# Seven places of weights and projection inputs, each at its own offset modulo 256 bytes

## The chip, the cores and the metric

The kernel runs on one core of a Trainium2 chip. The metric is the device time of one execution in microseconds; the time before is the median of three runs. The profile is one further execution, taken by the hardware profiler.

## The reference

A decoder trunk of two layers over 1024 tokens of width 1024, all in float32. Each layer mixes the tokens with three groups of heads side by side:

```
mod = SiLU(c) @ W_mod + b_mod;  shift, scale, gate = split(mod)
h = RMSNorm_pre(x) * (1 + scale) + shift
proj = h @ W_in                      # 1024 x 3088, split into the inputs of three groups
  A: sliding-window attention (window 128, 8 heads, 2 key/value heads, rotary, sinks)
  B: retention (4 heads, chunks of 128, own rotation and decay)
  C: gated linear attention (4 heads, low-rank data-dependent decay)
every group's output * SiLU(its gate path); B and C RMS-normalised per head first
y = concat(A, B, C) @ W_out          # 1024 x 1024
x = x + gate * RMSNorm_post(y)
```

## The kernel before

**Two halves of a number.** The large products (h @ W_in and the mix @ W_out) run in float32r, TensorE's one-pass form of a four-byte number. To keep float32's accuracy each operand is split into a high part (rounded to float32r) and a low part (the rest), and three products are added: high by high, low by high, high by low. In the code this is `PASSES = ((0, 0), (1, 0), (0, 1))`, over which `accum` loops, and inside it over eight blocks k of 128 rows of the contraction; so a product has 24 matmuls into one PSUM tile `mm`, each with another stationary operand of 128x128. Every matmul goes through the helper `mult` (line 171), every transpose through `transp` (line 186).

**Seven places.** Weights and projection inputs live in two long SBUF tiles, `arena0` and `arena1`, cut into seven places: 0, 1 and 2 in arena0, 3 to 6 in arena1. A place holds both halves of a weight unit of 256 columns (`unit`), or both halves of the transposed input h of two token tiles (`hT`): 2 x 8 rows of 256 four-byte numbers in each partition, 16384 bytes. Places 0 and 2 are wider (17408 bytes) since the unit rv has 16 more columns and is kept with rows of 272 numbers, 1088 bytes. `place(i)` gives the view of a place; the table `PLACES` has the tile, the offset in four-byte elements and the width of each. `TOK` says which places hold h in each layer (1, 2, 3, 4 in the first, 3, 4, 0, 1 in the second), `PLACE` which unit of weights goes where: rv, gg, gqk, aq0 and ag1 into place 0 (layer 0) or 2 (layer 1); rg, rk, gv, aq1 and o2 into 5; rq, kv, ag0 and o3 into 6; o0 and o1 into the first two places of h, once h is done with.

**Which operand moves.** `project` streams 256 columns of one unit (272 for rv) against h of one token tile; `project2` streams two units of 256 columns each as one moving operand of 512, joined by `both`, which steps from one place to the other; `project_T` streams h of two places (512 tokens) against 128 columns of a unit; `y_half` streams two units of W_out against `mx`, the mix of one token tile as read back from HBM (`load_mix`). In the last two token tiles of layer 1 the mix lies in a place of h instead. So in all of these the moving operand and the stationary one come from two different places, or from one or two places and mx.

**Where tiles stand.** SBUF is given out by pools that lie one above the other in each partition: const, big (arena0), work, and on top, once the start is over, big1 (arena1); a pool first, for the first modulation weights `wm`, has the room of arena1 before. The work pool has the working tiles: `sm` (small columns), `t1`, `kT`, `mx`, `t2` (14 buffers of 128x512), `acc`, `st` (staging of weights), `smx` and others. Two tiles that nothing reads or writes take up room alone: `pad` in const (96 bytes a partition) and `padw` in work (320 bytes). With them every place, and t1, kT, mx, t2, acc and st too, begin at multiples of 256 bytes.

**Order.** TensorE's instructions are in an order that the kernel writes out itself: the main loop issues the projections one product after another, and after every few matmuls `pump` lets waiting jobs (rotary, retention, attention, gates) issue their matmuls when a planner's clock says that they are due. The planner's clock and its latencies (table `L`) are constants of the program. The loads of weights (`load`) go through SP's queue into `st`; ScalarE and VectorE write the high half into its place and VectorE or GpSimd the low half (line 508).

Of the kernel before, what the change touches and what calls it, by code (L numbers as in the profile page):

```python
# [10 lines left out]
F32 = mybir.dt.float32  # L11
F32R = mybir.dt.float32r
# [5 lines left out]
P = 128  # L18
# [24 lines left out]

SLOT = KT * 512
WIDE = KT * 544
PLACES = {0: (0, 0, 272), 1: (0, WIDE, 256), 2: (0, WIDE + SLOT, 272)}
PLACES.update({3 + i: (1, i * SLOT, 256) for i in range(4)})
TOK = ((1, 2, 3, 4), (3, 4, 0, 1))
PLACE = []
for _t, _w in zip(TOK, (0, 2)):  # L50
# [39 lines left out]
def trunk(ctx: ExitStack, tc: tile.TileContext, ins, cst, out):  # L90
# [8 lines left out]
    bp = ctx.enter_context(tc.tile_pool(name="big", bufs=1))  # L99
    gp = ctx.enter_context(tc.tile_pool(name="work", bufs=2))  # L100
    ps = ctx.enter_context(tc.tile_pool(name="psum", bufs=3, space=bass.MemoryType.PSUM))
    dr = ctx.enter_context(tc.tile_pool(name="dram", bufs=1, space=bass.MemoryType.DRAM))

    gp.tile([P, 80], F32, tag="pad", name="padw", bufs=1)
    uid = [0]

    def nm(s):
# [21 lines left out]
    def f(ap):  # L129
        return ap.bitcast(F32)  # L130

    arenas = [bp.tile([P, 2 * WIDE + SLOT], F32R, name="arena0")]

    def place(i, w=256):
        n, o, _ = PLACES[i]
        return arenas[n][:, o:o + 2 * KT * w].rearrange("p (a k n) -> p a k n", a=2, k=KT)
# [623 lines left out]
    with tc.tile_pool(name="first", bufs=1) as wp:  # L760
        mod_first(rws, between)
    ap = ctx.enter_context(tc.tile_pool(name="big1", bufs=1))
    arenas.append(ap.tile([P, 4 * SLOT], F32R, name="arena1"))
    if XF:
        for t in (2, 3):
            load_x(t, xe[t], nc.sync)
# [540 lines left out]
    def load_mix(l, t):  # L1307
# [6 lines left out]
        if l == DEPTH - 1 and t in MIXP:  # L1314
            n, o, _ = PLACES[TOK[l][t // 2]]
            o += t % 2 * 2 * KT * P
# [323 lines left out]
```

## Time and profile before

| | |
|---|---|
| median of 3 runs | 957.99 us (956.76 to 958.2) |
| profiled execution | 954.65 us |
| its span | 952.9 us |
| granted TensorE clock | 0.997 |
| TensorE busy (matmul) | 932.7 us, 98% |
| weight loads | 770.1 us, 81% |
| VectorE, ScalarE, GpSimd | 67%, 50%, 23% |
| DMA | 142.26 MB, 149 GB/s in the mean |

Busy times are unions of an engine's instructions; since matmuls are pipelined, the time of one (its mean in ns) is longer than the step from one to the next. PE stands for TensorE's matmuls, PEld for its weight loads, DVE for VectorE, ACT for ScalarE, POOL for GpSimd, SP for the queue of SyncE.

### The profile page before, as it was taken

To read this page: it belongs to the slowest core of one execution; us is meant where nothing else is said; L and a number is where in the kernel's file an instruction comes from. 1 tells how busy PE (TensorE), PEld (TensorE's weight loads), DVE (VectorE), ACT (ScalarE), POOL (GpSimd) and SP (SyncE) were. 2 spreads that over 40 slices of the span, in tenths; PEclk is the share of its full clock that TensorE was granted. 3 is DMA by queue.
4 is the path that set the end of the run, shared out by engine and by line. 5 is a ranking of instruction groups with operands and counts; after the bars stand their busy time and mean duration, and the time that the engine had idled before them with its cause. 6 is when DMAs were issued, how large, how long until landed. Compare 5 with 4: busy or idle time off the path is not lost.

```text
span 952.9 us, 15951 instructions
## 1 busy us (share of the span) xinstructions
PE 932.7 (98%) x5645; PEld 770.1 (81%) x5645; DVE 637.4 (67%) x1372; ACT 474.1 (50%) x1157; POOL 222.6 (23%) x288
## 2 busy tenths in 40 slices
PE   5999999999999999999999999999999999999997
PEld 1799887888888787778889888888888887787886
DVE  6886857757786988654685584694677787862332
ACT  3786233554756666622455532443667576661111
POOL 3222000423231324510131110033133033540000
PEclk9999999999999999999999999999999999999999
DMA  9943523613362345787455261362133222555951
GB/s 320 323 135 122 161 84 122 196 49 115 107 200 80 100 133 189 226 253 256 171 169 175 92 187 32 101 187 67 56 101 111 94 82 81 166 177 177 308 200 66
DMA packets 124651, 142.26 MB, mean 149 GB/s; under 512 B 11566, under 2 KB 95384, under 8 KB 124572
## 3 DMA queue, kind: packets, MB, share of 16 engines
q1 hardware_dynamic: 114396, 127.43, 42.1%
q10 hardware_dynamic: 10176, 13.82, 4.2%
q8 instruction: 44, 0.72, 0.3%
q14 instruction: 35, 0.29, 0.1%
HBM read 104.51 MB, written 36.70 MB: 148 GB/s over the span
## 4 chain that ended last, share of the span: by engine, by line
PE 85%; DVE 3%; issue 2%; ACT 2%; POOL 0%; DMA 0%; DVEq 0%; SPq 0%; POOLq 0%; ACTq 0%
PE mm L171 67%; PE aux L171 14%; PE aux L186 4%; ACT smx L971 0%; DMA t<-tabS 0%; ACT L1026 0%; DVE t L856 0%; ACT L1025 0%; DVE t L1029 0%; DVE t L1027 0%; DVE t L157 0%; ACT mx L1160 0%; DVE smx L966 0%; DVE arena L508 0%; DVE arena L149 0%
## 5 line engine op out<-in xcount | busy, mean ns | idle before, releaser
L171 PE MATMUL mm<-arena,arena 128*128 128x512 f32 (+2 forms) x1512 | 309.6, 358 | 0.0
L171 PE MATMUL mm<-arena 128*128 128x512 f32 (+2 forms) x1392 | 285.8, 359 | 0.0
L171 PEld LDWEIGHTS mm<-arena,arena 128*128 128x128 f32 x1512 | 246.5, 189 | 40.1 <-issue 2.1
L171 PEld LDWEIGHTS mm<-arena 128*128 128x128 f32 x1392 | 228.9, 190 | 37.2 <-issue 1.2
L171 PE MATMUL mm<-arena,mx 128*128 128x512 f32 (+1 forms) x696 | 157.3, 384 | 0.0
L171 PEld LDWEIGHTS mm<-arena,mx 128*128 128x128 f32 x696 | 126.5, 188 | 26.1 <-issue 1.5
L508 POOL TENSOR_TENSOR arena<-st,arena 128x512 fp32r<-128x512 f32 x57 | 85.9, 1512 | 158.0 <-ACT arena L147 100.3
L147 ACT ACTIVATE t<-aux 128x512 f32<-128x512 f32 x64 | 37.1, 591 | 82.6 <-PE aux L186 39.6
L508 DVE TENSOR_TENSOR arena<-st,arena 128x512 fp32r<-128x512 f32 x63 | 63.0, 1014 | 6.9 <-ACT arena L147 3.5
L147 ACT ACTIVATE arena<-st 128x512 fp32r<-128x512 f32 x82 | 48.4, 623 | 31.1 <-PE mm L171 15.0
L1285 ACT ACTIVATE t<-mm 128x512 f32<-128x512 f32 x30 | 17.9, 598 | 91.0 <-PE mm L171 46.3
L971 ACT ACTIVATE smx<-smx,sm 128x129 f32<-128x129 f32 x128 | 50.1, 394 | 18.1 <-DVE sm L968 17.9
L975 POOL TENSOR_TENSOR smx<-smx,sm 128x512 f32<-128x512 f32 x32 | 35.2, 1099 | 82.5 <-DVE sm L974 78.7
L384 DVE SCALAR_TENSOR_TENSOR acc<-st,c_act,acc 128x512 f32<-128x512 f32 x60 | 45.6, 760 | 13.1 <-DMA st<-in_w_mod_dram 12.1
L562 POOL TENSOR_TENSOR sm<-sm,few 128x1 f32<-128x1 f32 x26 | 14.8, 570 | 150.3 <-DVE sm L561 147.6
L1286 DVE TENSOR_TENSOR t<-mm,modg 128x512 f32<-128x512 f32 x30 | 20.7, 689 | 42.4 <-ACT t L1285 42.4
L1330 DVE SCALAR_TENSOR_TENSOR t<-t,sm,t 128x512 f32<-128x512 f32 x32 | 25.5, 827 | 30.8 <-DMA t<-xs 15.7
L186 PE MATMUL aux<-c_ident,t 128*128 128x128 f32 x224 | 33.7, 274 | 4.1 <-DVE t L634 2.3
L186 PEld LDWEIGHTS aux<-c_ident,t 128*128 128x128 f32 x224 | 26.6, 140 | 10.5 <-DVE t L634 2.7
L966 DVE COPY_PREDICATED smx<-c_curmask,aux 128x256 f32<-128x256 int32 x64 | 25.5, 447 | 12.8 <-ACT smx L147 11.4
L370 POOL MEMSET acc<- 128x512 f32 x4 | 2.1, 529 | 130.2 <-PE aux L171 119.1
L851 DVE TENSOR_TENSOR t<-mm,sincos 128x128 f32<-128x128 f32 (+2 forms) x36 | 16.2, 450 | 23.7 <-ACT t L147 12.5
(223 smaller groups left out, 1340.5 us busy)
## 6 DMA issues: line engine op xcount, KB each, us to landing
st<-in_w_in_dram SPq DMA_DIRECT2D x96, 256.0 KB, 3.9
st<-in_w_mod_dram SPq DMA_DIRECT2D x64, 256.0 KB, 3.0
mixS<-t SPq DMA_DIRECT2D x64, 256.0 KB, 2.5
mx<-mixS SPq DMA_DIRECT2D x28, 512.0 KB, 5.2
st<-in_w_out_dram SPq DMA_DIRECT2D x32, 256.0 KB, 3.2
wm<-in_w_mod_dram SPq DMA_DIRECT2D x12, 512.0 KB, 4.7
t<-in_x_dram SPq DMA_DIRECT2D x24, 256.0 KB, 4.9
t<-tabS SPq DMA_DIRECT2D x16, 256.0 KB
```

Of the source, the lines that this page charges most:

```text
L147: A.activation(dst, src, AF.Copy)
L171: T.matmul(dst, lhsT, rhs, start=start, stop=stop)
L186: T.transpose(dst, src, idn)
L384: V.scalar_tensor_tensor(acc, wt, c_act[:, k:k + 1], acc, ALU.mult, ALU.add)
L508: i = (G if first == 0 and kc in LOG else V if first == 0 else eng(f"wlo{kc}")).tensor_tensor(wt[:, 1, 2 * kc:2 * kc + 2, 0:256], st, f(hi ...
L851: V.tensor_tensor(a4, s4, cs.unsqueeze(1).unsqueeze(1).to_broadcast((P, nh, 2, 32)), ALU.mult)
L966: V.copy_predicated(sv, curmask.unsqueeze(1).to_broadcast((P, 2, P)), pv[:, :, n // P - 1, :])
L971: A.activation(sm[:, h, :], sm[:, h, :], AF.Exp, bias=mx[:, h:h + 1], accum_out=sums[:, h:h + 1])
L975: eng("pn").tensor_tensor(sm[:, :, 0:128], sm[:, :, 0:128], rs.unsqueeze(2).to_broadcast((P, 4, P)), ALU.mult)
L1285: A.activation(yg, pm, AF.Square, accum_out=ss[:, nh:nh + 1])
L1286: V.tensor_tensor(yg, pm, modg[l][:, 512 * nh:512 * nh + 512], ALU.mult)
L1330: V.scalar_tensor_tensor(xt[j], yg[j], r, xt[j], ALU.mult, ALU.add)
```

## The change

The offsets of the seven places get an addend, given in four-byte elements (`SHIFT`): 0, 4, 8, 12, 24, 28 and 60, which is 0, 16, 32, 48, 96, 112 and 240 bytes. arena0 is 8 elements longer and arena1 60. The tile `padw` of 320 bytes is dropped from the work pool, and a tile `pad1` of 32 bytes is put ahead of arena1. So arena0 and arena1 themselves still begin at multiples of 256 bytes, and the working tiles in between come 288 bytes lower.

```diff
 SLOT = KT * 512
 WIDE = KT * 544
-PLACES = {0: (0, 0, 272), 1: (0, WIDE, 256), 2: (0, WIDE + SLOT, 272)}
-PLACES.update({3 + i: (1, i * SLOT, 256) for i in range(4)})
+SHIFT = (0, 4, 8, 12, 24, 28, 60)
+PLACES = {0: (0, 0, 272), 1: (0, WIDE + SHIFT[1], 256), 2: (0, WIDE + SLOT + SHIFT[2], 272)}
+PLACES.update({3 + i: (1, i * SLOT + SHIFT[3 + i], 256) for i in range(4)})
...
-    gp.tile([P, 80], F32, tag="pad", name="padw", bufs=1)
...
-    arenas = [bp.tile([P, 2 * WIDE + SLOT], F32R, name="arena0")]
+    arenas = [bp.tile([P, 2 * WIDE + SLOT + 8], F32R, name="arena0")]
...
     ap = ctx.enter_context(tc.tile_pool(name="big1", bufs=1))
-    arenas.append(ap.tile([P, 4 * SLOT], F32R, name="arena1"))
+    ap.tile([P, 8], F32, name="pad1")
+    arenas.append(ap.tile([P, 4 * SLOT + 60], F32R, name="arena1"))
```

## The prediction

> **What bounds the kernel now.** I read the page first (busy times, clock, chain), then who waits for TensorE's operands, then the groups by shape, then single runs of matmuls in the timeline.
>
> ```profile
> span 952.9 us, 15951 instructions
> PE 932.7 (98%) x5645; PEld 770.1 (81%) x5645; DVE 637.4 (67%) x1372; ACT 474.1 (50%) x1157; POOL 222.6 (23%) x288
> PEclk9999999999999999999999999999999999999999
> ...
> PE 85%; DVE 3%; issue 2%; ACT 2%; POOL 0%; DMA 0%; DVEq 0%; SPq 0%; POOLq 0%; ACTq 0%
> PE mm L171 67%; PE aux L171 14%; PE aux L186 4%; ACT smx L971 0%; DMA t<-tabS 0%; ACT L1026 0%; DVE t L856 0%; ACT L1025 0%; DVE t L1029 0%; DVE t L1027 0%; DVE t L157 0%; ACT mx L1160 0%; DVE smx L966 0%; DVE arena L508 0%; DVE arena L149 0%
> ...
> PE aux L186 <- DVE posr L425: 6.1, 1, 6.1
> PE aux L186 <- DVE t L634: 2.3, 1, 2.3
> PE aux L186 <- DVE smx L966: 1.7, 3, 0.9
> PE aux L186 <- ACT t L632: 1.1, 1, 1.1
> ```
>
> TensorE is busy for 98% of the span at full clock, carries 85% of the chain that ended last, and waits for nobody for more than a few us in all, most of it at the start. So what counts is how fast TensorE goes through its own list. 67% of the chain is the matmuls into mm, which read the places that the change moves. Their shapes:
>
> ```profile
> L171 PE MATMUL mm<-arena,arena 128*128 128x512 f32 x984 | 241.5, 397 | 0.0
> L171 PE MATMUL mm<-arena 128*128 128x512 f32 x912 | 223.1, 396 | 0.0
> L171 PE MATMUL mm<-arena,mx 128*128 128x512 f32 x648 | 151.3, 392 | 0.0
> L171 PE MATMUL mm<-arena,arena 128*128 128x256 f32 x336 | 43.6, 285 | 0.0
> L171 PE MATMUL mm<-arena 128*128 128x256 f32 x288 | 36.2, 284 | 0.0
> L171 PE MATMUL mm<-arena 128*128 128x272 f32 x192 | 27.3, 302 | 0.0
> L171 PE MATMUL mm<-arena,arena 128*128 128x272 f32 x192 | 25.3, 290 | 0.0
> L171 PE MATMUL mm<-arena,mx 128*128 128x256 f32 x48 | 6.2, 284 | 0.0
> ...
> L171 PE MATMUL aux<-acc,c_ones 128*128 128x512 f32 x8 | 4.1, 592 | 0.0
> ```
>
> That is 984 + 912 + 648 = 2544 matmuls of 512 columns, 336 + 288 + 48 = 672 of 256, and 384 of 272: 3600 in all, each with a weight load of its own. What one costs in a stream, start to start, shows in long unbroken runs of the timeline (start, length to the last one's end, how many):
>
> ```profile
> 871.20 53.79 PE L171 MATMUL mm<-arena,mx 128*128 128x512 f32 x236
> ...
> 71.38 5.91 PE L171 MATMUL mm<-arena 128*128 128x256 f32 x48
> ...
> 77.13 4.91 PE L171 MATMUL mm<-arena,arena 128*128 128x272 f32 x38
> ...
> 500.45 10.10 PE L171 MATMUL mm<-arena,arena 128*128 128x272 f32 x79
> ...
> 775.08 7.53 PE L171 MATMUL mm<-arena,arena 128*128 128x512 f32 x32
> ```
>
> Take the last one's own time off the length and divide by the number of steps. 512 columns: (53.79 - 0.39) / 235 = 227.2 ns. 256 columns: (5.91 - 0.28) / 47 = 119.8 ns. The difference is 107.4 ns for 256 columns, 0.42 ns a column, so 512 columns stream in 214.8 ns, and **about 12.4 ns of every step are no streaming**, for both widths alike. The plain f32 matmuls on acc and c_ones do not show them: four pairs are busy 4.1 us, 1.025 us a pair, less 0.592 for the second one leaves 0.433 us for two passes over 512 columns, 430 of it streaming at that rate. So the 12.4 ns belong to these fast one-pass matmuls (float32r), whose stream reads four bytes per column time while the next 128 columns of weights are read. A stall of the stream by that weight read, some 30 column times long, is the reading that I take; whether the two reads collide could then depend on where they start. That, and nothing else on the path, is what the change can move.
>
> **The change part by part.** *Where everything stands.* By the allocator's sums, before, all seven places, t1, t2, st, mx and kT begin at multiples of 256 bytes in each partition. After, the places stand at 0, 16, 32, 48, 96, 112, 240 past one. The 320-byte pad of the work pool goes and arena0 grows by 32, so t1, t2, st, mx and kT come 288 bytes lower, to 224 past a multiple; pad1 (32 bytes) makes that up for arena1. No instruction, DMA, wait or queue is added, removed or moved; the order on every engine is written out as before.
>
> *Stream against weights (the 3216 matmuls of 512 and 256 columns).* Before, the start of the moving operand and that of the weights always agree modulo 256. After, no pair does. In bytes, moving less stationary modulo 256: o2 and o3 (places 5 and 6, the two halves of one moving operand) against mx 144 and 16 (312 matmuls), places 1 and 2 against 0: 16 and 32 (192), 3 and 4 against 0: 48 and 96 (192), 3 and 4 against 2: 16 and 64 (192), 5 and 6 against 1: 96 and 224 (120). The trace of before has one place where this varies: the rv projection's 272 columns make rows of 1088 bytes, so its moving start walks on by 64 bytes with each k: 0, 64, 128, 192 past the weights' residue. At 0.42 ns a column 272 columns would take 114.1 + 12.4 = 126.5 ns if the overhead were that of the others. Its two runs give (4.91 - 0.29) / 37 = 124.9 and (10.10 - 0.29) / 78 = 125.8 ns: 1.6 and 0.7 below, 1.1 in the mean over four residues of which one (0) is the old one. If only the unequal ones gain, that is 1.1 x 4/3 = 1.5 ns for each; if only the odd multiples of 64 do, 2.2 ns. Ends: a gain of the whole 12.4 ns (f32 has it), and a loss of 3.1 ns, which is what the 32 matmuls at 775.08 cost each over the long run's 227.2, (7.53 - 0.39) / 31 = 230.3, a run that begins after other work and has the same addresses; so the overhead also depends on how the two reads fall in time, and unequal starts can hit a worse phase too. I take **2.0 ns**, near the 272s, the only rows with unequal starts: 3216 x 2.0 = 6.4 us off.
>
> *The 384 matmuls of 272 columns* walk through the residues already: 0; with 1 ns either way, 0.4 us.
>
> *Transposes and the other matmuls into aux.* After, ident (224 past) and the t2 tiles have equal residues, which were 224 apart. The smx tiles are 129 wide, so that their four heads begin 516 bytes apart, at many residues:
>
> ```profile
> 774.29 1.04 PE L186 MATMUL aux<-c_ident,smx 128*128 128x128 f32 x8
> ...
> 486.58 1.03 PE L186 MATMUL aux<-c_ident,t 128*128 128x128 f32 x8
> ```
>
> Eight of either take the same time: 0. A difference of 1 ns over some 2000 such records would be 2 us.
>
> *DVE, ScalarE, GpSimd, whose tiles move by 32 modulo 256:* 0 on the path, since TensorE covers them; the fullest window is
>
> ```profile
> 0.00:40.00 40.00, 29.39 (x121) 14.77 (x122) 30.21 (x62) 18.61 (x45) 12.74 (x32) 0.96 0.97 344
> 300.00:400.00 100.00, 98.32 (x618) 78.12 (x617) 80.96 (x150) 66.46 (x200) 37.82 (x41) 1.00 0.45 141
> ```
>
> with DVE (third count) busy for 81% there. If that cover went with a faster TensorE, a stage such as this would give back what it gained, 0.7 us per 100. *DMA:* the first 40 us have the 16 engines busy for 97%; rows that land 224 past a multiple of 256 instead of on it cost nothing by my estimate, since ident and ones land there already; 1% more there would be 0.4 us, and elsewhere the share of 45% covers it.
>
> Sum: 6.4 off and nothing back. The profiled execution took 954.65 us for its span of 952.9, so 948.2 for that one; the median of the three runs, 957.99, stands 3.3 above it, so **951.6 us**, a change of -0.7%. About 0.2%, or 1.9 us, is what a measurement of this kernel tells from no change.
>
> One rule of the Trainium skill speaks against all this: TensorE: Matmul & The Clock Gate, section Step-by-step: what each phase is for, says that the moving operand and the weights have independent read ports and that "Loading the next tile's weights doesn't steal SBUF read bandwidth from the running matmul". By it the sum is 0 and the time 958.0. The 12.4 ns beside 0.433 us for f32 do not look like it, but no run here has taken the weight load away, so it stays a rival with a chance below. The same page's section Back-to-back issue gap gives N / 2.4 + 2.5 ns, 215.8 for 512 columns; by that figure the most there is to gain is 11.4 ns a matmul in place of my 12.4.
>
> **The rivals.** *No change (958.0).* The 12.4 ns are a fixed cost of swapping weights, not a collision. For it: they are the same for 256 and 512 columns, for one moving segment and for two, and for pairs in one arena and in two. Against it: the 272s come out 0.7 to 1.6 ns lower, and the same matmul costs 230.3 in one run and 227.2 in another. Chance 0.20.
>
> *Slower.* Equal starts are the good phase: the long runs sit at 227.2 undisturbed, and only after a switch of work is the step longer. With starts of 16 to 240 bytes apart each pair of places settles somewhere else, and each change of pair (every 24 matmuls) starts a new settling. At the 3.1 ns of the 775.08 run this gives 3216 x 3.1 = 10.0 us, 968; it decides for slower from 0.6 ns in the mean (1.9 us / 3216). Against it are the 272s, which change residue with every step and are still no dearer than the rest. Chance 0.22; 960 to 968.
>
> *Much faster.* If unequal starts take away half of the 12.4 ns, 3216 x 6.2 = 19.9 us go and the time is 938; all of it would be 918. For it is only f32; against it the 272s, which at three residues of four lose a tenth. Chance 0.12 from 941 down to there.
>
> **How the numbers follow.** Forecast, a gain between 1.9 and 17 us: 0.46, its own range 945 to 956. With the much faster case, 0.58 for faster by over 0.2%; 0.20 for within; 0.22 for slower. The range 941 to 966 leaves out most of the much faster case and the last of the slower one, under 2 in 10 together.
>
> **What would show it.** Right: the 512-column run at the end (o2, o3, o0, o1 of layer 1 against mx) goes from 227.2 to about 225 ns a step, the 256-column runs from 119.8 to about 118, and the busy times of the eight arena groups fall together by some 6 us, with DVE, ScalarE and GpSimd durations as before. The mean of one matmul (389 to 397 now) would fall by the same 2 ns, since a stalled stream shows there too. Wrong: runs at 227.2 still (a fixed cost), steps that differ from pair to pair with some above 230 (phases), shorter steps with new waits of TensorE on DVE around 300 to 400 us, or longer DVE and GpSimd instructions on the moved tiles.

## The result, and the profile after

The changed kernel takes 966.48 us (median of 4 runs, 966.34 to 966.74), the kernel before 958.1 in the same comparison (4 runs, 956.76 to 960.79): a ratio of 1.0085, interval 1.0069 to 1.0102. It is slower by 8.4 us; the forecast was 951.6, 6.4 us faster. The profiled execution of after took 966.74 us.

The page of after, its first lines and the chain:

```profile
span 965.0 us, 15950 instructions
PE 942.1 (98%) x5645; PEld 768.4 (80%) x5645; DVE 637.3 (66%) x1372; ACT 473.6 (49%) x1157; POOL 221.0 (23%) x288
PEclk9999999999999999999999999999999999999999
...
PE 80%; DVE 4%; ACT 4%; issue 3%; DMA 1%; POOL 1%; DVEq 0%; SPq 0%; POOLq 0%; ACTq 0%
```

TensorE is still 98% busy at full clock and still carries the chain. VectorE, ScalarE, GpSimd and the weight loads are as busy as before to within 2 us. Only the busy time of the matmuls has grown, 932.7 to 942.1. The groups by shape of after (busy us, mean ns of one, then idle time before them) show where:

```profile
L171 PE MATMUL mm<-arena,arena 128*128 128x512 f32 x984 | 244.9, 400 | 0.0
L171 PE MATMUL mm<-arena 128*128 128x512 f32 x912 | 226.3, 399 | 0.0
L171 PE MATMUL mm<-arena,mx 128*128 128x512 f32 x648 | 154.3, 396 | 0.0
L171 PE MATMUL mm<-arena,arena 128*128 128x256 f32 x336 | 43.8, 285 | 0.0
L171 PE MATMUL mm<-arena 128*128 128x256 f32 x288 | 35.0, 279 | 0.0
L171 PE MATMUL mm<-arena 128*128 128x272 f32 x192 | 26.1, 292 | 0.2 <-ACT arena L708 0.2
L171 PE MATMUL mm<-arena,arena 128*128 128x272 f32 x192 | 25.6, 290 | 0.1
L171 PE MATMUL mm<-arena,mx 128*128 128x256 f32 x48 | 6.1, 281 | 0.0
```

The three 512-column groups were 241.5 + 223.1 + 151.3 = 615.9 us and are 625.5: **+9.6 us**. The 256s were 86.0 and are 84.9: -1.1. The 272s were 52.6 and are 51.7: -0.9, which is mostly the clock at the start and not their steps (experiment 2). Together +7.6 of the 8.4 that the medians differ by. No wait has come: the idle time ahead of these groups is 0.3 us in all.

The same in the timeline of after (start, length, how many), the runs that answer to those shown of before, in their order:

```profile
881.41 55.13 PE L171 MATMUL mm<-arena,mx 128*128 128x512 f32 x236
...
73.72 5.62 PE L171 MATMUL mm<-arena 128*128 128x256 f32 x48
...
79.18 4.91 PE L171 MATMUL mm<-arena,arena 128*128 128x272 f32 x38
...
505.49 10.42 PE L171 MATMUL mm<-arena,arena 128*128 128x272 f32 x79
...
784.05 7.71 PE L171 MATMUL mm<-arena,arena 128*128 128x512 f32 x32
```

The 236 matmuls against mx took 227.2 ns a step and take (55.13 - 0.40) / 235 = 232.9. The 32 that stood out before with 230.3 take (7.71 - 0.40) / 31 = 235.8. The 48 of 256 columns went the other way, 119.8 to (5.62 - 0.28) / 47 = 113.6. The 272s stand at 124.9 as before in one run and at (10.42 - 0.29) / 78 = 129.9 instead of 125.8 in the other. Below, "settled" is the mean step, start to start in the trace, of the matmuls from the 21st step of a series on, or beyond the 12th consecutive one inside the kernel. Before, 512 columns settle at 226.7 for every pair of places and 256 at 120.0; after, the larger groups of pairs lie between 229.4 and 233.4, one small group at 242.

### The profile page after: what moved, and what is told of

The parts are those of the page before. It is cut to its first block, busy times and chain, and to the rows that moved or that the text cites. A ratio compares the mean times of both kernels' runs of the same rounds, so it can differ in the third digit from the quotient of the medians.

```text
span 965.0 us, 15950 instructions
## 1 busy us (share of the span) xinstructions
PE 942.1 (98%) x5645; PEld 768.4 (80%) x5645; DVE 637.3 (66%) x1372; ACT 473.6 (49%) x1157; POOL 221.0 (23%) x288
## 4 chain that ended last, share of the span: by engine, by line
PE 80%; DVE 4%; ACT 4%; issue 3%; DMA 1%; POOL 1%; DVEq 0%; SPq 0%; POOLq 0%; ACTq 0%
PE mm L171 63%; PE aux L171 14%; PE aux L186 3%; DVE t L1028 0%; ACT t L147 0%; DVE arena L149 0%; DMA t<-in_x_dram 0%; DVE t L1030 0%; DVE arena L508 0%; ACT L1026 0%; DVE t L1331 0%; ACT mx L1162 0%; ACT smx L972 0%; ACT t L654 0%; DMA t<-tabS 0%
## 5 line engine op out<-in xcount | busy, mean ns | idle before, releaser
L171 PE MATMUL mm<-arena,arena 128*128 128x512 f32 (+2 forms) x1512 | 313.5, 361 | 0.1
L171 PEld LDWEIGHTS mm<-arena 128*128 128x128 f32 x1392 | 226.3, 188 | 40.5 <-issue 1.2
L171 PE MATMUL mm<-arena,mx 128*128 128x512 f32 (+1 forms) x696 | 160.2, 388 | 0.0
L508 POOL TENSOR_TENSOR arena<-st,arena 128x512 fp32r<-128x512 f32 x57 | 83.4, 1468 | 161.6 <-ACT arena L147 113.8
L508 DVE TENSOR_TENSOR arena<-st,arena 128x512 fp32r<-128x512 f32 x63 | 59.9, 962 | 6.8 <-ACT arena L147 3.5
L186 PEld LDWEIGHTS aux<-c_ident,t 128*128 128x128 f32 x224 | 27.3, 143 | 11.9 <-DVE t L634 3.7
L654 ACT ACTIVATE t<-aux,mod,mod 128x128 f32<-128x128 f32 x56 | 21.2, 454 | 23.5 <-PE aux L186 21.6
```

The source lines that it names most:

```text
L171: T.matmul(dst, lhsT, rhs, start=start, stop=stop)
L186: T.transpose(dst, src, idn)
L508: i = (G if first == 0 and kc in LOG else V if first == 0 else eng(f"wlo{kc}")).tensor_tensor(wt[:, 1, 2 * kc:2 * kc + 2, 0:256], st, f(hi ...
L654: A.activation(hf[:, ks], pt[:, ks], AF.Identity, scale=gain, bias=shift)
```

## The experiments

**Theories.** *Phase:* what counts is by how many bytes modulo 256 the moving operand starts past the weights; equal starts are the lowest step of a 512-column matmul, others cost. *Alignment:* a place that is not on a multiple of 256 (or 64) bytes costs, whatever the other operand does. *Tiles:* the working tiles, 288 bytes lower after, cost. In the kernels below that keep all of the computation, the offset of a place or of a tile is all that differs; the sweeps add matmuls behind the kernel whose results nobody uses.

**1. The work pool alone: the change with all seven addends at 0.**

```diff
-SHIFT = (0, 4, 8, 12, 24, 28, 60)
+SHIFT = (0, 0, 0, 0, 0, 0, 0)
```

> The change with all seven offsets at 0: the places begin at multiples of 256 bytes again, only the working tiles (mx, t1, t2, st) stay 224 bytes past. Theory of tiles (the moved working tiles are what costs): 966. Theory of phases (what counts is moving start less weights' start modulo 128 or 256): only the matmuls against mx, where the two now differ by 32, go from 227 to some 231 ns, 648 x 4 = 2.6 us, 960 to 961, and all others keep 226.7. Theory of alignment (what counts is where a moving segment begins, by itself): only stationary operands moved, 958.

963.98 us, ratio 1.006 (1.0045 to 1.0076). Its 512-column groups:

```profile
L171 PE MATMUL mm<-arena,arena 128*128 128x512 f32 x984 | 241.3, 396 | 0.0
L171 PE MATMUL mm<-arena 128*128 128x512 f32 x912 | 223.1, 396 | 0.0
L171 PE MATMUL mm<-arena,mx 128*128 128x512 f32 x648 | 155.0, 397 | 0.0
```

Place against place, still equal, is unchanged (241.5 and 223.1 before). Only the matmuls against mx lost, 151.3 to 155.0 us: mx stands at 224 past, the places on the multiple, 32 bytes apart. They settle at 233.3 ns instead of 226.7. So equal starts hold, and a move of mx alone breaks them.

**2. Everything moved together: 32 bytes more ahead of all that follows, all starts stay equal.**

```diff
-    cp.tile([P, 24], F32, name="pad")
+    cp.tile([P, 32], F32, name="pad")
```

> The kernel before with 32 bytes more of padding at the bottom of each partition, so that all places and all working tiles begin 32 bytes past a multiple of 256 and all starts still agree with one another. Theory of phases: 958, the long 512-column runs at 226.7 ns. Theory of alignment: every moving segment begins 32 past, so the 512-column matmuls go to 231 to 233 ns as in the changed kernel, 966 or more.

959.45 us, ratio 1.0012 (0.9998 to 1.0026): no change that can be told. Groups:

```profile
L171 PE MATMUL mm<-arena,arena 128*128 128x512 f32 x984 | 241.5, 397 | 0.0
L171 PE MATMUL mm<-arena 128*128 128x512 f32 x912 | 223.1, 396 | 0.0
L171 PE MATMUL mm<-arena,mx 128*128 128x512 f32 x648 | 151.6, 392 | 0.3 <-DMA mx<-mixS 0.3
...
L171 PE MATMUL mm<-arena 128*128 128x272 f32 x192 | 26.1, 292 | 0.3 <-ACT arena L708 0.3
```

With every place and tile 32 bytes past a multiple of 256 the 512s are as before: alignment falls, as far as 32 bytes go (the sweeps have a case of 16). The 272s, whose addresses relative to their weights are the same as before too, went from 27.3 (302 ns) to 26.1 (292) all the same. That is not their steps. In the profile of before some of them fall into a stretch with a granted clock of 0.50 (TensorE's busy time and count, then clock and DMA):

```profile
35.30:38.60 3.30, 3.30 (x17) 0.50 1.03 346
```

Fourteen of them step 227 ns there; in experiment 2 no such stretch falls on them. Settled, the long runs of the 272s step alike in both, 125.1 (38 matmuls) and 125.8 (79).

**3 and 4. Places 5 and 6, then place 6 alone, 64 bytes on.**

Both against the kernel before, so that the working tiles stay where they were; the fence has the third, and the fourth differs in its first line, (0, 0, 0, 0, 0, 0, 16).

```diff
-PLACES = {0: (0, 0, 272), 1: (0, WIDE, 256), 2: (0, WIDE + SLOT, 272)}
-PLACES.update({3 + i: (1, i * SLOT, 256) for i in range(4)})
+SHIFT = (0, 0, 0, 0, 0, 16, 16)
+PLACES = {0: (0, SHIFT[0], 272), 1: (0, WIDE + SHIFT[1], 256), 2: (0, WIDE + SLOT + SHIFT[2], 272)}
+PLACES.update({3 + i: (1, i * SLOT + SHIFT[3 + i], 256) for i in range(4)})
...
-    arenas.append(ap.tile([P, 4 * SLOT], F32R, name="arena1"))
+    arenas.append(ap.tile([P, 4 * SLOT + 16], F32R, name="arena1"))
```

> The kernel before with places 5 and 6 alone moved, both by 64 bytes, working tiles as before. Theory of phases: all 672 matmuls of 256 columns see starts 64 apart and go from 119.8 to 113.6 ns, as those with 64 and 192 apart did in the changed kernel, -4 us; the 1392 matmuls of 512 columns with 5 or 6 in them (both halves of the moving operand equal) gain too if the half column time matters alone, 4 to 6 ns each, -6 to -8; so 945 to 950. Theory of alignment: the 912 that stream 5 and 6 lose 5 ns each if 64 counts as unaligned (+4.6 us), the 256s gain 4: 958. The pair places 1, 2 against 0 is the control: 226.7 in both.

> The kernel before with place 6 alone moved by 64 bytes, so that the two halves of the moving operand from 5 and 6 begin at unequal residues (0 and 64 past the weights). Theory of phases with the first half alone deciding: these 912 stay at 226.7, the matmuls against weights in 6 (192) gain; with the 256-column ones of 6 (some 340 at 113.6) 955. A third theory, unequal halves: a jump from one half to the other between unequal residues upsets the phase at every step, these 912 go to 230 to 233 ns, +3 to +6 us, 958 to 962, although neither half does so alone.

960.79 us, ratio 1.0034 (1.0021 to 1.0047), and 963.43, ratio 1.0054 (1.0037 to 1.007). Place 6 alone costs no less than 5 and 6 together. The gain that the theory of phases was expected to bring in the third kernel (945 to 950) did not come: the 256s gained, but the 512s lost at 64 and at 192 bytes alike. The 512s settle at 229.6 ns where both halves of the moving operand are 64 past the weights, at 232.8 with the halves 0 and 64 past, at 233.4 where h moves against weights 64 past it (192 apart), and at 227 in the pairs left equal. The 256s gain: 113.6 at 192 apart, 117.7 at 64, 120.0 when equal. One group of each, third kernel and then fourth, shows the halves:

```profile
L172 PE MATMUL mm<-arena,mx 128*128 128x512 f32 x648 | 152.5, 394 | 0.0
```

```profile
L172 PE MATMUL mm<-arena,mx 128*128 128x512 f32 x648 | 153.2, 395 | 0.0
```

Before, 151.3: o2 and o3 against mx lose 1.2 us at (64, 64) and 1.9 at (0, 64).

**5. The places alone: the change, but mx, t1, t2, st and kT back on multiples of 256.**

```diff
+    gp.tile([P, 8], F32, tag="pad", name="padw", bufs=1)
...
-    ap.tile([P, 8], F32, name="pad1")
```

> The places stand at 0, 16, 32, 48, 96, 112 and 240 past a multiple of 256 as in the changed kernel, but mx, t1, t2, st and kT stay at multiples of 256. If the steps of the matmuls on the places carry the loss: the pairs place against place are as after, those of a place against mx are unequal in other amounts, the mean 512-column step is 236 to 237 ns against 233.0 before, the ratio to before 1.0065 to 1.009. If the 288 bytes by which the working tiles moved cost by themselves (about 1 to 2 us of the kernel with the work pool alone moved were not in its steps), the ratio is lower than the changed kernel's by that, 1.005 to 1.0065. If the place moves cost nothing (all the loss from the working tiles), 1.000 to 1.002.

966.39 us, ratio 1.008 (1.0068 to 1.0093), the changed kernel's own. Groups:

```profile
L172 PE MATMUL mm<-arena,arena 128*128 128x512 f32 x984 | 244.6, 400 | 0.0
L172 PE MATMUL mm<-arena 128*128 128x512 f32 x912 | 226.3, 399 | 0.0
L172 PE MATMUL mm<-arena,mx 128*128 128x512 f32 x648 | 154.5, 397 | 0.0
```

So the places alone give the whole loss, and the two parts do not add: 1.006 for the pool and 1.008 for the places make 1.0085 together. Once a pair is unequal, making it unequal in another way costs little more (154.5 against mx here, 154.3 after, 155.0 in experiment 1). Working tiles that cost by themselves are not seen: this kernel and the changed one, which differ in them alone, take 966.39 and 966.48 us. Tiles falls, but for what mx does as an operand.

The accounts of these kernels against the profile of before, in us, from the sums of the groups by shape:

| kernel | 512s | 256s | 272s | sum | measured ratio |
|---|---|---|---|---|---|
| after | +9.6 | -1.1 | -0.9 | +7.6 | 1.0085 |
| 1 work pool alone | +3.5 | +0.1 | -1.2 | +2.4 | 1.006 |
| 2 all 32 past | +0.3 | +0.3 | -1.1 | -0.5 | 1.0012 |
| 3 places 5, 6 | +4.6 | -1.9 | +0.1 | +2.8 | 1.0034 |
| 4 place 6 | +5.4 | -0.2 | -1.3 | +3.9 | 1.0054 |
| 5 places alone | +9.5 | -1.0 | -1.1 | +7.4 | 1.008 |

The order is the measured one but for experiment 1, and the sums fall short by 0.3 to 1.7 us, in experiment 1 by 3.3 (5.7 measured, its interval 4.3 to 7.3; 0.1% is 0.96 us). Two things in these sums are no steps. The column of the 272s is mostly the half clock at the start, which falls on them in the profiles of before and of experiment 3 and not in the others. And the profiled execution of before is a short one of its kind, 954.65 against a median of 958: its first matmul on a place starts at 31.8 us, those of the other profiles at 32.9 to 34.1. Experiment 2 has the steps of before without both, so its profile is the better measure: against it the spans are longer by 8.0 us (after), 3.4 (1), 4.6 (4) and 7.5 (5), and the sums by 8.1, 2.9, 4.4 and 7.9. In the profiles, then, the steps make up the loss; only experiment 3 is off, 1.1 against 3.3. The profile of experiment 1 is the shortest of its four executions, 962.12 against a median of 963.98; the rest of what its median lost is not explained.

**6 to 8. Sweeps of the start addresses by themselves.** Behind the kernel before, series of 48 matmuls on places 1 (weights), 3 and 4 (moving), with the letter a to p for j = 0 to 15, 16 bytes each:

```
eq: 512 columns, both halves 16 j past the weights' start
se, fi: only the second, only the first half 16 j past
na: 256 columns, 16 j past
on: 512 columns in one piece, 16 j past
ab: moving and weights both at 16 j
we: the weights at 16 j, moving at 0
hf: 64 columns of weights;  sa: one column read 128 times as weights
by: 4 j bytes past;  wi: 512 to 64 columns, equal starts
ze: one moving column read 512 times;  st: the same k at every step
tw: the same 256 columns twice;  hw: 256 columns, the weights at 16 j
```

> The kernel before with extra work behind it that nothing uses: series of 48 matmuls each, both operands from the places, weights' start at 0 past a multiple of 256, moving start at 16 j bytes past, j = 0 to 15 (tiles named a to p in that order). eq: 512 columns in two halves, both at 16 j; se: first half at 0, second at 16 j; na: 256 columns at 16 j. Only the steps inside a series count, not the time of the kernel. Phases: eq a 226.8 ns, eq c 233 (seen with 32), eq e 230 and eq m 233 (seen with 64 and 192), na a 120, na e and na m 114 to 118; if the period is 128 bytes, i to p repeat a to h. Unequal halves: every se but a above 230, although the first half agrees with the weights. If only the first half counted, all se 226.8.

> The kernel before with other series of 48 matmuls behind it. on: 512 columns in one piece at 16 j bytes past, no jump inside: with the theory of phases about as eq, with the theory of the jump all near 226.8. fi: second half at 0, first at 16 j. ab: moving halves and weights all at 16 j, j = 0, 1, 2, 4, 8: 226.8 in all if only the difference counts. hf: weights of 64 columns (half of the output rows left out), j = 0, 2, 4, 8: if the 12.4 ns are a stall by the weight read they go to about half, 221 at j = 0; if they are a fixed price of a swap, 226.8. by: starts 0, 4, 8, 12 bytes past: 226.8 in all if 16-byte lines count. sa: the weights are one column read 128 times: if the stall comes from lines of memory that collide, the step changes from 226.8 and no longer depends on j.

> The kernel before with series of 48 matmuls behind it whose results nothing uses. The first reading of the 226.7 ns (a fixed 12.4 ns for each matmul on a stream of 0.42 ns a column) stands against a second one: the stream itself runs at 0.4427 ns a column when nothing stalls it (226.7 / 512, and 113.3 / 256, the lowest step seen with any starts), so 512 columns with equal starts have no stall at all and only the 256s have one. wi a to h: one piece of 512, 448, ... 64 columns, equal starts: first reading 214.8 + 12.4 falling by 26.9 for each 64 columns, 200.3, 173.5, ... 119.8 at 256; second reading steps on a line through the origin where there is no stall, 198.3 at 448, 170.0 at 384. ze: 512 times the same column: if reading from memory sets the rate, well under 226.7. tw: the same 256 columns twice. st: the same row k at every step (no walk through the place). we: moving at 0, weights at 16 j: if only the difference counts, we b = eq p = 226.7, we p = eq b = 231.6. hw: the same with 256 columns, 113.3 at some j.

Timeline of the first sweep (eq at 0, 16, 32, 160 and 240 bytes; na at 0, 112 and 192):

```profile
951.08 11.07 PE L1592 MATMUL eqa<-arena,arena 128*128 128x512 f32 x48
961.99 11.28 PE L1592 MATMUL eqb<-arena,arena 128*128 128x512 f32 x48
973.11 11.37 PE L1592 MATMUL eqc<-arena,arena 128*128 128x512 f32 x48
...
1062.24 11.41 PE L1592 MATMUL eqk<-arena,arena 128*128 128x512 f32 x48
...
1118.34 11.05 PE L1592 MATMUL eqp<-arena,arena 128*128 128x512 f32 x48
...
1305.68 5.90 PE L1592 MATMUL naa<-arena,arena 128*128 128x256 f32 x48
...
1345.58 5.60 PE L1592 MATMUL nah<-arena,arena 128*128 128x256 f32 x48
...
1373.75 5.62 PE L1592 MATMUL nam<-arena,arena 128*128 128x256 f32 x48
```

In 10.7 us of steps (11.07 - 0.39) the equal series is shortest but for eqp, 240 past. Settled, eq takes 226.7 ns at 0 and at 240 and between 228.9 and 234.6 elsewhere; se, fi and we lie between 226.7 and 236.7, and no series of 512 columns with a walking stream (one that goes from address to address) is lower than 226.7. The 256s take 120.0 when equal, 116.6 to 119.9 mostly, and 113.3 at 112 and 192. One piece (on) gives the same as two halves at every j, within 0.1 ns, so the jump between the places is free.

From the second sweep, both operands at 128 past (ab), the moving operand 4 bytes past (by), and one column as weights at 0 and at 32 past (sa):

```profile
1350.74 11.08 PE L1592 MATMUL abi<-arena,arena 128*128 128x512 f32 x48
...
1416.72 11.68 PE L1592 MATMUL byb<-arena,arena 128*128 128x512 f32 x48
...
1450.60 11.15 PE L1592 MATMUL saa<-arena,arena 128*128 128x512 f32 x48
1461.58 11.28 PE L1592 MATMUL sac<-arena,arena 128*128 128x512 f32 x48
```

Both at 32, 64 or 128 settle at 226.7 as both at 0 do; both at 16 takes 230.0. Four bytes apart is the dearest of the sweeps, 240.0. Half as many weight columns (hf) take 229.6, 230.9, 228.4 and 229.2 at 0, 32, 64 and 128, and weights read from one single column (sa) 228.9 at 0 and 231.6 at the three others, where full weights take 226.7, 233.3, 228.9 and 232.6. So the excess does not shrink with the number of weight columns, as a stall by the weight read was expected to (221 for hf); but the spread between the starts shrinks, which no run here explains.

From the third sweep, the narrow end of wi (128 and 64 columns) and ze, in the timeline and in windows (TensorE's busy time and count, the weight loads', the others', then the granted clock):

```profile
997.22 5.50 PE L1592 MATMUL wig<-arena,arena 128*128 128x128 f32 x48
1002.55 7.57 PE L1592 MATMUL wih<-arena,arena 128*128 128x64 f32 x48
1009.94 13.53 PE L1592 MATMUL zea<-arena,arena 128*128 128x512 f32 x48
```

```profile
1010.00:1014.00 4.00, 4.00 (x11) 3.18 (x11) 0.00 (x0) 0.00 (x0) 0.00 (x0) 0.50 0.00 0
...
1018.00:1023.00 5.00, 5.00 (x25) 4.38 (x24) 0.00 (x0) 0.00 (x0) 0.00 (x0) 1.00 0.00 0
```

Back at full clock, ze settles at 215.9 ns, 10.8 below the walking stream with equal starts, with the weights loaded each time as ever. So the excess goes when the stream does not walk through memory; it is no fixed price of swapping weights.

Of the two readings that this sweep was to tell apart, the widths with equal starts (wi) bear out the first, a fixed excess on a stream of 0.42 ns a column: 120.0, 146.7 and 173.3 ns at 256, 320 and 384 columns and 226.7 at 512 lie on one line, 0.417 ns a column and 13.3 over (the second reading gave 170.0 at 384). Only 448 columns lie off it, 202.7 for 200.0. The same 256 columns twice (tw) and the same row at every step (st) give what eq gives at 0, 32 and 64: 226.7, 233.3, 228.9. And a weights' start 240 past (we), a difference of 16 like that of eqb, takes 226.7 and not 231.6: already here the difference alone does not fix the step.

**9. Does the sweep carry over?** The units rk, rq, gv and kv, when they move, start 240 past the h that stands as weights (226.7 for 512 columns in the first sweep); rg of layer 0 stands 64 past the h that moves against it (192 apart); everything else is equal. Pads make the room; their lines are left out here.

```diff
-PLACES.update({3 + i: (1, i * SLOT, 256) for i in range(4)})
+PLACES.update({5: (1, 4, 256), 6: (1, SLOT + 68, 256)})
+PLACES.update({3 + i: (1, (2 + i) * SLOT + 72, 256) for i in range(2)})
+SHIFT = dict(rk=0, gv=0, rq=0, kv=0, rg=4, aq1=4, o2=4, ag0=4, o3=4)
...
+        return place(PLACE[l][name], 272 if name == "rv" else 256,
+                     20 if (l, name) == (0, "rg") else SHIFT.get(name, 0))
```

> An arrangement by unit of weights in place of one by place: units that only ever move against h (rk, rq, gv, kv) begin 240 past the others, rg of layer 0 (256 columns of h moving against it) 64 past, everything else equal. By the sweep 512 columns at 240 are as good as at 0 (226.7), 256 columns take 117.1 at 240 and 113.3 at 192, against 120.0 at 0. 192 matmuls x 6.7 + 384 x 2.9 = 2.4 us less than before, 955.7 for 958.1 (0.9975). If the sweep's steps do not carry over to the kernel, where other work stands between the runs: 958.

961.19 us, ratio 1.0027 (1.0015 to 1.0038): slower, no gain. The 256s came as in the sweep (117.1 and 113.6, 1.5 us less by their groups), but the 512s at 240 apart settle at 235.1 ns inside the kernel, not at 226.7, and the 512s lost 3.1 us. A difference of starts alone does not fix the step.

**10. What ran ahead.** 48 matmuls of 512 columns at 240 (xa), 0 (xb), 64 (xc) and 144 bytes (xd), each behind eight other kinds of work (a to h).

```diff
+    for name, j in (("xa", 15), ("xb", 0), ("xc", 4), ("xd", 9)):
+        for i, ahead in enumerate((lambda: plain(128), lambda: plain(64), lambda: eq("un", 0), lambda: eq("un", 2),
+                                   lambda: eq("un", 5), lambda: narrow(0), lambda: narrow(7), lambda: narrow(12))):
+            N_ = 16
+            ahead()
+            N_ = 48
+            eq(name + LET[i], j)
```

> 32 series of 48 matmuls of 512 columns are added behind the kernel, with both halves of the moving operand 240 (xa), 0 (xb), 64 (xc) and 144 bytes (xd) past the weights' start; ahead of each stand 16 matmuls of another kind (plain f32 of 128 and 64 columns; 512 columns at 0, 32, 80; 256 columns at 0, 112, 192). If the start addresses alone fix the step, every one of the eight settles where the first sweep had it: xa 226.7 ns, xb 226.7, xc 228.9, xd 233.3, each within 0.5. If an unequal pair has several rhythms and what runs ahead decides which one it falls into, at least xa spreads by 2 ns or more over the eight (the kernel with rk, rq, gv and kv 240 past had 235.1 where the sweep had 226.7), while equal starts (xb) stay at 226.7 in all eight. No series under 226.5 by either.

Timeline, xa behind 512 columns at equal starts and at 80 bytes; xb behind the same equal ones; xc behind 256 columns at equal starts and at 112:

```profile
984.09 11.36 PE L1592 MATMUL xac<-arena,arena 128*128 128x512 f32 x48
...
1013.92 11.52 PE L1592 MATMUL xae<-arena,arena 128*128 128x512 f32 x48
...
1097.54 11.04 PE L1592 MATMUL xbc<-arena,arena 128*128 128x512 f32 x48
...
1251.19 11.37 PE L1592 MATMUL xcf<-arena,arena 128*128 128x512 f32 x48
...
1264.27 11.16 PE L1592 MATMUL xcg<-arena,arena 128*128 128x512 f32 x48
```

The same addresses settle in different rhythms: xa at 233.3 (two of eight) or 236.7 (six), in neither case at the first sweep's 226.7; xc at 228.9 (seven) or 233.3 (one, behind the 256s at equal starts). Equal starts (xb) settle at 226.7 in all eight, xd at 233.3 in all eight. So a pair of unequal starts may have several settled steps. Which PSUM buffer is written does not decide it: three take turns, and xaa and xad write the same one, as do xac and xaf. What ran before is the one thing left that differs. Each series ran once; that it is no chance rests on series such as on, which repeat eq's steps in another run. It is the likely reason for the miss of experiment 9.

**11. The one unit that only ever has 256 columns of h moving against it: rg of layer 0, 64 bytes on.** Place 6 and a pad make the room; their lines are left out.

```diff
+        return place(PLACE[l][name], 272 if name == "rv" else 256, 16 if (l, name) == (0, "rg") else 0)
```

> The kernel before, with the unit rg of layer 0 alone 64 bytes later in its place: its 192 matmuls of 256 columns stream it against the weights' start in h 64 bytes apart, everything else stays equal. By the sweep (256 columns against weights 64 bytes on: 113.3 ns; in the kernels 113.6 settled against 119.8) those steps go from 120 to about 114: 192 x 6 ns = 1.2 us off, ratio 0.9988, 0.998 to 1.000 by this. If the start of other matmuls shifts with it, or the 256s settle elsewhere, 1.000 or above. All other steps as before: 512 columns settled at 226.8.

958.37 us, ratio 0.9997 (0.9988 to 1.0006). The two groups that hold these 192 matmuls:

```profile
L172 PE MATMUL mm<-arena,arena 128*128 128x256 f32 x336 | 43.1, 284 | 0.0
L172 PE MATMUL mm<-arena 128*128 128x256 f32 x288 | 35.6, 281 | 0.0
```

43.6 + 36.2 became 43.1 + 35.6: the 1.1 us came (settled 113.5 instead of 120.0, the 512s at 226.7 as before), but in the time it cannot be told from nothing. It is the only layout tried that is not slower in the middle of its interval, and no version that beats the kernel before.

## Why the prediction was wrong

**What bounds the kernel: right.** Only the steps of the matmuls on the places moved. TensorE's waits sum to 16.7 us after and to 17.2 in experiment 2, which is no slower; no other engine is busier.

**The excess of 12.4 ns as a stall of the walking stream: supported in part.** Its size holds: 13.3 ns at equal starts, for 256 and 512 columns alike (wi). The series that does not walk steps at 215.9 (215.8 is the estimate by the Trainium skill's formula for the gap of an isolated matmul, TensorE: Matmul & The Clock Gate, section Back-to-back issue gap; here the trace agrees) and the equal walking one at 226.7, so about 10.8 ns are the walk. That it is the weight read which the stream meets is not shown: a weight load of half the columns, or of a single column, did not lower it.

**Stream against weights, 3216 x 2.0 ns off: the step that failed.** It took equal starts for the place where the two reads collide, which unequal ones relieve, and carried the gain of the 272s over to the 512s. The sign is wrong for 512 columns. Equal starts are the lowest step that 512 columns have here (226.7, none below it in the sweeps while the stream walks), so unequal starts had nothing to relieve. They cost 9.6 us over 2544 matmuls, 3.8 ns each. Only the 256s have something to gain, up to 6.7 ns at 112 and 192 bytes, and as the places lie, 672 of them gained 1.1 us, 1.6 ns each. That this is near the 2.0 forecast is luck: their pairs settle anywhere between 113.3 and 120.0.

The 2.0 came from the 272s. What the prediction read of them holds as far as it goes: by the line of wi 272 columns with equal starts would take 126.7 ns, an estimate, and the two runs settle at 125.1 and 125.8, in experiments 2 and 3 too. (The group of 272s with 302 ns in its rows, dearer than the rest, is the half clock at the start.) But they are near the 256s in width, not the 512s, and the two widths went opposite ways. No row of before had 512 columns with unequal starts, so for 2544 of the 3216 matmuls the sign was open.

**The loss of 3.1 ns a matmul, the other end of the range, was misread.** The 32 matmuls at 775.08 average 230.3 against the long run's 227.2 at the same addresses, but not because each of them is dearer. Two parts of that run, in the trace of before:

```profile
775.08 1.86 PE L171 MATMUL mm<-arena,arena 128*128 128x512 f32 x7
...
776.55 6.05 PE L171 MATMUL mm<-arena,arena 128*128 128x512 f32 x26
```

The first six steps, behind the transposes, take (1.86 - 0.39) / 6 = 245 ns, the first of all 314; the last 25 take (6.05 - 0.39) / 25 = 226.4, no more than in the long run. It is the price of an entry, some 110 ns once. The rival "Slower" took it for each of 3216 matmuls, 10.0 us and 968. Measured: +3.8 on the 512s, -1.6 on the 256s, 2.6 over all 3216, and 966.48; that its price came so near is luck. What it had right is the mechanism: equal starts are the good phase, and each unequal pair settles somewhere else. The runs add that the pairs stay there, many of them in a repeating pattern of two or three steps (226, 229, 232 for xc). The range stopped at 966.0, short of the 968 that this rival gives by its own sum.

**No change (a fixed cost of swapping weights):** falls, by 215.9 in ze and by steps that differ from pair to pair. The Trainium skill's rule of independent ports (same page, Step-by-step: what each phase is for) would have given 958.0. The trace does not agree with a time that is free of where the weights stand: the series "we" moves nothing but the weights' start and goes from 226.7 to 233.4 at 32 bytes.

**Transposes, other engines, DMA at 0:** right to within what the profiles tell. The eight kinds of matmuls into mm make up 7.6 us, and the places alone (experiment 5) make up the ratio without any move of the working tiles.

**Open:** which two accesses collide; why the lowest 512-column step is 226.7 and not 215.9; and which entry leads to which rhythm. No run took the weight load away from a walking stream. One row bears on it: in the stretch of half clock at 35.3 us the 272s walk and load weights each time, and step 227 ns, which is 272 columns at 0.833, twice the 0.417 of wi, with nothing over.

## What to carry to other kernels

Where float32r matmuls of 512 columns fill TensorE, let the moving operand and the weights begin at the same offset modulo 256 bytes, itself a multiple of 32 (both at 0, 32, 64 or 128 took 226.7, both at 16 took 230.0); of four differences tried behind eight kinds of work only this one always settled at the lowest step, and 32 bytes ahead of everything cost nothing that could be measured. Before an effect is carried from one shape to another, look for a row of that shape that has it; here there was none for 512 columns, and one series of 48 would have told the sign. Before the mean of a run is taken as the price of a step, take its entry apart from its settled steps. And a sweep of one parameter tells what a layout can do, not what it does inside a kernel, as long as what ran before has a say.

## What the runs showed of the hardware that was not expected

- A shift of 4 bytes between stream and weights cost most in the sweeps, 240.0 ns a step against 226.7; 8 bytes 235.6, 12 bytes 230.0.
- 512 and 256 columns have opposite preferences: at 192 bytes apart 256 columns gain 6.7 ns and 512 lose 6.7 (120.0 to 113.3, 226.7 to 233.4).
- The two commonest settled steps of 512 columns, 226.7 and 233.3, lie 6.7 ns apart, and so does the dearest of the sweeps, 240.0, from the second; for 256 columns it is 113.3 and 120.0.
- Below 256 columns a step stops shrinking: 192 columns 111.7 ns, 128 columns 111.6, with 128 columns of weights loaded each time.
- The series of 64 columns, behind those of 192 and 128, was slowed in mid-series: its steps went from 112 to 213 ns, and the window at 1010 us shows a granted clock of 0.50; it came back after some 10 us, in the series of 512 columns that followed.
